# A hybrid decoder trunk: the experts' loop written out in slots of a weight tile, and score products of two heads alternated

## The chip, the core and the metric

The kernel runs on one core of a Trainium2 chip. The metric is the device time of one execution in microseconds, as the median of several. The engines' names in the rows are PE (TensorE's products), PEld (its weight loads), DVE (VectorE), ACT (ScalarE), POOL (GpSimd) and SP (the queue that issues the loads).

## What is computed

Two layers over 256 tokens of width 1024, in float32. Each layer adds a mixer, a cross attention over 256 memory tokens and a feed-forward part to `x`. The mixer has three groups: 4 mLSTM heads, a convolution over 31 taps, and 8 "FoX" heads, a causal attention whose logits get a sum of log forget gates. All heads are 64 wide. The second layer's feed-forward part is a mixture of 8 experts, of which each token uses two:

```python
def forgetting_attention(q, k, v, log_f):
    ...
        logits = jnp.einsum("bhqd,bhkd->bhqk", qi, kh) + ci[..., None] - c[:, :, None, :]
        logits = jnp.where(pi[:, None] >= kpos[None, :], logits, -jnp.inf)
        p = jax.nn.softmax(logits, axis=-1)
        return jnp.einsum("bhqk,bhkd->bhqd", p, vh)

def swiglu(h, w_gate, w_up, w_down):
    a = jnp.einsum("bsd,df->bsf", h, w_gate)
    u = jnp.einsum("bsd,df->bsf", h, w_up)
    return jnp.einsum("bsf,fd->bsd", jax.nn.silu(a) * u, w_down)

def moe_swiglu(h, router_w, w_gate, w_up, w_down):
    logits = jnp.einsum("bsd,de->bse", h, router_w).astype(jnp.float32)
    top_v, top_i = lax.top_k(logits, TOP_K)
    top_w = jax.nn.softmax(top_v, axis=-1)
    gates = jnp.sum(jax.nn.one_hot(top_i, N_EXPERTS, dtype=jnp.float32) * top_w[..., None], axis=-2)
    y = jnp.zeros(h.shape, jnp.float32)
    for e in range(N_EXPERTS):
        y = y + gates[..., e:e + 1] * swiglu(h, w_gate[e], w_up[e], w_down[e]).astype(jnp.float32)
```

The inner width of an expert is 2816. In the mLSTM too the scores of a head are products of queries and keys over 64 channels, weighted by gates.

## The kernel before

**Weights.** All weights come from memory in tiles of 128 x 2048 float32 (1 MB), in one list that `weight_order` makes. `load` (L150) takes a free staging tile and issues the load on SP; the staging has four tiles (`STAGES[0]`), for the experts three more (`STAGES[1]`) and the spare tiles named `wsp`, four of them. A product is exact enough only when its operands are split into a high part of fewer bits and the rest: `halve` (L159) makes from a tile the high half `wh` by a ScalarE copy (L165) and the low half `wl` by a VectorE subtraction (L169), each in two pieces of 128 x 1024; a staging tile is free again after its last subtraction. `w(key)` (L193) hands out the next tile of the list and lets the splitting run `split_ahead` = 2 tiles ahead.

**Experts.** The experts are worked through in eight places, 0 to 7. The tokens that belong to an expert are gathered by products with one-hot matrices `oh`, and its results are scattered back by products with the transposed ones. The even places are long, with 128 token slots: `expert` (L1194) with three products for each piece of weights (`mm3`: low x high, high x low, high x high). The odd places are short, with 64: `short` (L1234) puts the high and the low half of its tokens side by side into 128 columns, so that two products do. Each expert has 11 chunks of 256 inner channels; a chunk needs three weight tiles, two of gate and up (`eg`, 8 pieces of 512 columns) and one of down (`ed`, 4 pieces). After the products with gate and up of a chunk, a long expert does the silu (`es`, L1228), the product with up (L1229), two transposes (`et`, L1201) and the split `ehh`, `ehl`. A short one copies the result (`eg`, ACT L1276), adds the two halves and turns them in one go by products with `comb` (`et`, L1246), and then does silu (`es`, L1248), product (L1249) and split (L359, L363). The products with down follow a chunk or two later.

**What sets the order.** The code of a chunk is written as one flow; `behind` (L1155) lets turns, down products and scatters of earlier chunks come one chunk later each, and `at(fc)` (L1325) starts the gather of the next group of places (`prepare`, L1284) at chunk 3 and goes on with it, two of the eight columns per chunk. From this flow a scheduler makes each engine's order of instructions, by priority and by what it reckons to be ready. Each engine then runs its instructions in that fixed order and waits where an input is not there.

**Attention.** `attend` calls `scores(h)` for each head in turn. In `fox` (L658) this makes for each of two query blocks i a product of queries and keys (L668, 64 rows, 128 or 256 columns), the gate bias (L669) and the causal mask (L670), all added up in one PSUM tile `fs`. The heads 2p and 2p+1 lie in the two halves of the 128 rows of `fq` and `fk`. `mlstm` (L737) does its two score products (L755, 256 columns; L756, 128) for one head after the other.

Of the kernel before, what the change touches and what calls it, by code (L numbers as in the profile page):

```python
# [35 lines left out]
STAGES = (4, 3)  # L36
HALVES = 5
# [38 lines left out]
class Trunk:  # L76
# [7 lines left out]
    def __init__(self, ctx, tc, a, out):  # L84
        self.ctx, self.tc, self.nc, self.a, self.out = ctx, tc, tc.nc, a, out
        self.order = self.weight_order()
        self.loaded, self.ready = [], {}
        self.nload = self.nsplit = self.nused = 0
        self.mark = self.hold = self.kept = None
        self.split_ahead = 1  # L90
        self.cut = CUT[0]
        self.build()


    def weight_order(self):
# [3 lines left out]
        for l in range(DEPTH):  # L99
# [26 lines left out]
            lead = 3 if l % 2 == 0 else 6  # L126
# [31 lines left out]

    def halve(self, slot, st):  # L159

        nc, tc = self.nc, self.tc
        wh, wl = [Halves(*[self.wp.tile([P, 1024], F32R, name=n) for _ in range(2)]) for n in ("wh", "wl")]
# [37 lines left out]


    def build(self):
# [6 lines left out]
        self.wp = pool("wp", HALVES)  # L209
# [77 lines left out]
        with tc.tile_pool(name="emid", bufs=1) as self.md, tc.tile_pool(name="ewkb", bufs=2) as self.wb, \  # L287
                tc.tile_pool(name="wst2", bufs=STAGES[1]) as wst2:
            self.free += [slot(wst2)] * STAGES[1]
            
            self.xg = [self.big("xg", shape=(P, 2 * KD * P)) for _ in range(2)]
            self.spare()
            self.kept = self.spare()
            self.moe(0, 1)
# [363 lines left out]
    def fox(self, cat, fq, fk, fv):  # L658
        nc = self.nc
        po = {}  # L660

        def scores(h):
            hp, r = h // 2, slice((h % 2) * 64, (h % 2) * 64 + 64)
            ps = self.psum(name="fs")
            for i in range(NT):
                n = (i + 1) * P
                o = ps[:, 0:128] if i == 0 else ps[:, 128:384]
                nc.tensor.matmul(o, fq[r, hp, i * P:(i + 1) * P], fk[r, hp, 0:n], start=True, stop=False)  # L668
                nc.tensor.matmul(o, self.pick(4 + h), self.ahl[:, 0:n], start=False, stop=False)  # L669
                nc.tensor.matmul(o[:, n - P:n], self.identb, self.mask_up, start=False, stop=True)  # L670
            return ps, ((0, 128), (128, 384)), 1.0
# [64 lines left out]
    def mlstm(self, cat, qk, v1, so, nw):  # L736
# [5 lines left out]
        for h in range(5):  # L742
            if h < 4:
                r = slice((h % 2) * 64, (h % 2) * 64 + 64)
                q, kk = qk[r, h // 2, :], qk[r, 2 + h // 2, :]
# [8 lines left out]
                ps = self.psum(name="ms")  # L754
                nc.tensor.matmul(ps[:, 0:256], kk[:, 0:128], q, start=True, stop=True)  # L755
                nc.tensor.matmul(ps[:, 256:384], kk[:, 128:256], q[:, 128:256], start=True, stop=True)  # L756
# [334 lines left out]
    def moe(self, j, l):  # L1091
# [23 lines left out]
        def gather(lists, xg):  # L1115
# [8 lines left out]
            xr = wb.tile([P, len(lists)], F32, name=f"xr{len(lists)}")  # L1124

            def steps():
                for k in range(KD):
                    ks = slice(k * P, (k + 1) * P)
                    ps = self.psum(name="xg")
                    for s in range(2):  # L1130
                        for i in range(NT):
                            nc.tensor.matmul(ps[:, lo:lo + w], hm[1 - s][:, i, ks], ohs[:, i, lo:lo + w],
                                             start=s == 0 and i == 0, stop=s == 1 and i == NT - 1)
                    at = [slice(m * P + (C if short else 0), (m + 1) * P) for m, (_, short) in enumerate(lists)]
                    for t, c in zip(xg, at):
                        self.split_hi(t[:, k, 0], ps[:, c], norm.w[:, k:k + 1])
                    for t, c in zip(xg, at):
                        self.split_lo(t[:, k, 0], t[:, k, 1], ps[:, c], norm.w[:, k:k + 1])
                    if k % 2:
                        yield 1.0  # L1140
                ps = self.psum(name="xr")
                for m in range(len(lists)):
                    for i in range(NT):
                        nc.tensor.matmul(ps[:, m:m + 1], oh[:, i, m, :].bitcast(F32), rms[:, i:i + 1],
                                         start=i == 0, stop=i == NT - 1)
                nc.vector.tensor_copy(xr, ps[:, 0:len(lists)])
                yield 1.0

            return xg, xr, steps()


# [42 lines left out]
        def expert(gu, dn, x, xr, oh, gate, at=lambda fc: None, pre=()):  # L1194
# [22 lines left out]
            for fc in range(NFC):  # L1217
# [7 lines left out]
                if fc == 0:  # L1225
                    run(pre)
# [5 lines left out]
                at(fc)  # L1232

        def short(gu, dn, x, xr, oh, gate, at):  # L1234
# [3 lines left out]
            ps = [self.psum(name="ed") for _ in range(2)]  # L1238
# [4 lines left out]
            def turn(fc, g):  # L1243
                pt = self.psum((P, 4, C), "et")
                for b in range(4):
                    nc.tensor.matmul(pt[:, b, :], g[:, b * P:(b + 1) * P], comb, start=True, stop=True)  # L1246
                s = wb.tile([P, 256], F32, name="es")[:, 0:2 * C].rearrange("p (k t) -> p k t", t=C)
                nc.scalar.activation(s, pt[:, 0:2, :], AF.Silu)  # L1248
                nc.vector.tensor_tensor(s, s, pt[:, 2:4, :], op=ALU.mult)  # L1249
                h = wb.tile([P, 2, P], F32R, name="ehh", bufs=3).rearrange("p k (s t) -> p k s t", t=C)  # L1250
                self.split(h[:, :, 0, :], h[:, :, 1, :], s)
                later(lambda: down(fc, h))

            def down(fc, h):
                wh, wl = dn(fc)
                for n in range(2):
                    for k in range(2):
                        fs = slice(k * 1024 + n * 512, k * 1024 + (n + 1) * 512)
                        for w in (wl, wh):
                            nc.tensor.matmul(ps[n], h[:, k].rearrange("p s t -> p (s t)"), w[:, fs], start=fc == 0 and k == 0 and w is wl,  # L1260
                                             stop=fc == NFC - 1 and k == 1 and w is wh)
                if fc == NFC - 1:
                    evacuate(ps, oh, gate)

            for fc in range(NFC):
                pg = self.psum(name="eg")
                for hf in range(2):
                    wh, wl = gu(fc, hf)
                    for k in range(4):
                        c = hf * 4 + k  # L1270
                        fs = slice(k * 512, (k + 1) * 512)
                        for w in (wl, wh):
                            nc.tensor.matmul(pg, both[:, c], w[:, fs], start=c == 0 and w is wl,  # L1273
                                             stop=c == KD - 1 and w is wh)
                g = wb.tile([P, 512], F32, name="eg", bufs=1)
                nc.scalar.activation(g, pg, AF.Copy)  # L1276
                behind()
                turns.append(lambda fc=fc, g=g: turn(fc, g))
                at(fc)

        groups = {}
        lists = (pos, None)

        def prepare(n):  # L1284
# [3 lines left out]
            for i in range(NT):  # L1288
                for m, q in enumerate(places):
# [192 lines left out]
```

## Time and profile before

| what | value |
|---|---|
| median of 3 runs | 1386.63 us (1386.36 to 1388.93) |
| profiled execution, its own time | 1390.3 us |
| its span | 1388.5 us |
| PE busy | 1324.8 us, 95% of the span |
| DVE busy | 1175.7 us, 85% |
| ACT busy | 949.5 us, 68% |
| experts' loop, first product to last | 603.7 to about 1373 us |
| places 0 to 7 begin at | 603.7, 699.5, 783, 889.3, 978, 1080.5, 1171.2, 1274 us |

The busy shares are means over stages with different limits, so they are to be read by stretch. A place begins where its first gate and up product starts. The 1.8 us between span and own time lie around the span and are taken as given.

### The profile page before, as it was taken

Reading aid. Unit: us, or ns where it says so; the run is one execution under the profiler, and the core shown is the slowest. Engines: PE = TensorE matmul, PEld = TensorE weight load, DVE = VectorE, ACT = ScalarE, POOL = GpSimd, SP = SyncE. Lnnn points to the kernel's source line nnn. Section 1 sums busy time; section 2 is a strip of 40 time slices with the busy share of each in tenths; the row PEclk is TensorE's granted clock in tenths of the full one; section 3 lists DMA queues with packets and bytes.
Section 4 is the critical chain, followed back from the end, with each engine's and each line's share of the span. In section 5 each row is a group of like instructions: output and inputs, shape, how many; then the busy total and the mean of one; then the engine's idle time right before and its main releaser. Section 6 shows DMA issues by size and latency. Waiting matters only on the chain.

```text
span 1388.5 us, 20513 instructions
## 1 busy us (share of the span) xinstructions
PE 1324.8 (95%) x7257; PEld 1090.6 (79%) x7257; DVE 1175.7 (85%) x2059; ACT 949.5 (68%) x1501; POOL 8.1 (1%) x30
## 2 busy tenths in 40 slices
PE   9999999999999999989999989998999989999985
PEld 8878989999989778778886768866788766787663
DVE  7988876666678878689999989999999998989997
ACT  7565575444455555668799867878777787777884
POOL 0000100000000000000000000000000000000000
PEclk9999999999999999979999999999999999999998
DMA  8423626555544315669999988999999999999970
GB/s 315 173 73 116 217 92 213 182 184 185 190 177 152 122 61 182 237 235 343 337 373 391 421 323 321 353 382 380 370 347 335 357 367 389 333 341 361 337 300 33
DMA packets 67566, 368.05 MB, mean 265 GB/s; under 512 B 5744, under 2 KB 6000, under 8 KB 38016
## 3 DMA queue, kind: packets, MB, share of 16 engines
q1 hardware_dynamic: 67136, 365.59, 71.1%
q8 instruction: 59, 0.97, 0.3%
q0 software_dynamic: 320, 1.08, 0.2%
q14 instruction: 51, 0.42, 0.1%
HBM read 365.60 MB, written 1.05 MB: 264 GB/s over the span
## 4 chain that ended last, share of the span: by engine, by line
PE 71%; DVE 12%; DMA 10%; ACT 4%; issue 3%; DVEq 0%; SPq 0%; ACTq 0%
DVE wl L169 9%; PE fm L349 6%; PE fm L351 6%; PE fm L350 6%; PE eg L1273 6%; PE eg L350 5%; PE eg L349 5%; PE eg L351 5%; DMA wst<-in_moe_gu_dram 4%; DMA wst<-in_moe_w_down_dram 2%; ACT wh L165 2%; PE ed L349 2%; PE ed L351 2%; PE ed L350 2%; PE ed L1260 2%
## 5 line engine op out<-in xcount | busy, mean ns | idle before, releaser
L169 DVE TENSOR_TENSOR wl<-wst,wh 128x512 fp32r<-128x512 f32 (+1 forms) x668 | 614.0, 955 | 116.2 <-ACT wh L165 113.8
L165 ACT ACTIVATE wh<-wst 128x1024 fp32r<-128x1024 f32 x502 | 513.2, 1058 | 178.7 <-PE fm L351 90.8
L169 DVE TENSOR_TENSOR wl<-wsp,wh 128x1024 fp32r<-128x1024 f32 x188 | 222.7, 1221 | 18.8 <-ACT wh L165 16.7
L349 PE MATMUL fm<-hTh,wl 128*128 128x256 f32 x736 | 207.7, 282 | 0.7 <-DVE wl L169 0.7
L350 PE MATMUL fm<-hTl,wh 128*128 128x256 f32 x736 | 206.8, 281 | 0.0
L351 PE MATMUL fm<-hTh,wh 128*128 128x256 f32 x736 | 206.4, 280 | 0.0
L165 ACT ACTIVATE wh<-wsp 128x1024 fp32r<-128x1024 f32 x188 | 190.2, 1053 | 16.7 <-PE eg L351 7.5
L1273 PE MATMUL eg<-wl,xs 128*128 128x512 f32 x352 | 149.2, 424 | 12.2 <-DVE wl L169 11.6
L350 PE MATMUL eg<-wl,xg 128*128 128x512 f32 x352 | 141.9, 403 | 2.8 <-DVE wl L169 2.6
L349 PE MATMUL eg<-wh,xg 128*128 128x512 f32 x352 | 141.6, 402 | 0.0
L351 PE MATMUL eg<-wh,xg 128*128 128x512 f32 x352 | 140.0, 398 | 0.0
L349 PEld LDWEIGHTS fm<-hTh,wl 128*128 128x128 f32 x736 | 138.7, 188 | 1.6 <-DVE wl L169 0.9
L350 PEld LDWEIGHTS fm<-hTl,wh 128*128 128x128 f32 x736 | 138.6, 188 | 0.8 <-issue 0.2
L351 PEld LDWEIGHTS fm<-hTh,wh 128*128 128x128 f32 x736 | 138.9, 189 | 0.0
L1273 PE MATMUL eg<-wh,xs 128*128 128x512 f32 x352 | 138.4, 393 | 0.0
L1273 PEld LDWEIGHTS eg<-wl,xs 128*128 128x128 f32 x352 | 66.3, 188 | 41.5 <-DVE wl L169 19.0
L1260 PE MATMUL ed<-wl,ehh 128*128 128x512 f32 x176 | 76.7, 436 | 17.8 <-DVE wl L169 15.4
L350 PEld LDWEIGHTS eg<-wl,xg 128*128 128x128 f32 x352 | 66.9, 190 | 21.2 <-DVE wl L169 6.9
L349 PEld LDWEIGHTS eg<-wh,xg 128*128 128x128 f32 x352 | 67.0, 190 | 15.9 <-ACT wh L165 0.8
L351 PEld LDWEIGHTS eg<-wh,xg 128*128 128x128 f32 x352 | 66.7, 189 | 15.3
L1273 PEld LDWEIGHTS eg<-wh,xs 128*128 128x128 f32 x352 | 66.5, 189 | 10.0
L1260 PEld LDWEIGHTS ed<-wl,ehh 128*128 128x128 f32 x176 | 33.0, 187 | 48.7 <-DVE wl L169 35.9
(338 smaller groups left out, 2185.8 us busy)
## 6 DMA issues: line engine op xcount, KB each, us to landing
wst<-in_moe_gu_dram SPq DMA_DIRECT2D x114, 1024.0 KB, 7.0
wsp<-in_moe_gu_dram SPq DMA_DIRECT2D x62, 1024.0 KB, 7.0
wst<-in_moe_w_down_dram SPq DMA_DIRECT2D x56, 1024.0 KB, 6.9
wsp<-in_moe_w_down_dram SPq DMA_DIRECT2D x32, 1024.0 KB, 7.2
wst<-in_ffn_gu_dram SPq DMA_DIRECT2D x22, 1024.0 KB, 4.9
wst<-in_w_in_fm_dram SPq DMA_DIRECT2D x16, 1024.0 KB, 4.9
wst<-in_ffn_w_down_dram SPq DMA_DIRECT2D x11, 1024.0 KB, 5.0
wst<-in_w_in_tm_dram SPq DMA_DIRECT2D x8, 1024.0 KB, 5.2
```

The source lines that it names most:

```text
L165: self.halved = nc.scalar.activation(wh[:, s], st[:, s], AF.Copy)
L169: nc.vector.tensor_tensor(wl[:, s], st[:, s], wh[:, s].bitcast(F32), op=ALU.subtract)
L349: nc.tensor.matmul(out, ll, rh, start=start, stop=False)
L350: nc.tensor.matmul(out, lh, rl, start=False, stop=False)
L351: nc.tensor.matmul(out, lh, rh, start=False, stop=stop)
L1260: nc.tensor.matmul(ps[n], h[:, k].rearrange("p s t -> p (s t)"), w[:, fs], start=fc == 0 and k == 0 and w is wl, stop=fc == NFC - 1 and k ...
L1273: nc.tensor.matmul(pg, both[:, c], w[:, fs], start=c == 0 and w is wl, stop=c == KD - 1 and w is wh)
```

## The change

**Experts' loop.** In the loop of layer 1, ScalarE, VectorE and TensorE no longer get their order from the scheduler but from the order of the code (`manual_schedule`). The code is laid out in slots, one for each weight tile. `slot` issues in a fixed pattern: for ScalarE the steps posted at "act", the first half of the copy for the tile after next, the steps posted at "act mid", the second half; for VectorE half a subtraction for the next tile, the steps posted at "dve mid", the other half; for TensorE half of the tile's products, the steps at "pe mid", the other half, the steps at "pe". `post(n, where, step)` puts a small step into the slot n later. Silu, product, turn and split of a chunk, the scatter of a finished expert (`leave`), the gather of the next group (`spread`, one column per slot) and the norm weights for the end (`final_weights`) are posted like this. The down products of a chunk come after the gate and up products of the next.

**Buffers.** The staging has two tiles less (`STAGES` (4, 3) to (4, 1)), `wh` gets seven half tiles and `wl` six instead of five each, and the list of the experts' tiles begins with four gate and up tiles instead of six. The gather for place 0 runs as a whole before the loop; before, half of it came inside the first chunk.

**Scores.** In `fox` the two heads of a pair get their scores together, in two PSUM tiles: bias and mask of block 0 for both, the four products of queries and keys with the heads in turns, bias and mask of block 1. `mlstm` does the score products of two heads in turns as well.

```diff
-STAGES = (4, 3)
-HALVES = 5
+STAGES = (4, 1)
+HALVES = (5, {"wh": 2, "wl": 1})
...
-            lead = 3 if l % 2 == 0 else 6
+            lead = 3 if l % 2 == 0 else 4
...
+    def slot(self, key, *products):
+        t = self.nused
+        assert self.order[t][0] == key, (self.order[t][0], key)
+        self.now += 1
+        if t + 1 < len(self.order) and t + 1 >= self.nsplit and t + 1 not in self.parts:
+            self.high(t + 1, 0)
+            self.high(t + 1, 1)
+        self.places("act")
+        self.high(t + 2, 0)
+        self.low(t + 1, 0)
+        self.places("dve mid", "act mid")
+        self.high(t + 2, 1)
+        self.low(t + 1, 1)
+        w = self.ready.pop(key)
+        products[0](*w)
+        self.places("pe mid")
+        products[1](*w)
+        self.places("pe")
+        self.nused += 1
...
+            bias(0, True)
             for i in range(NT):
...
+                for k in range(2):
+                    r = slice(k * 64, k * 64 + 64)
+                    nc.tensor.matmul(out(k, i), fq[r, h // 2, i * P:(i + 1) * P], fk[r, h // 2, 0:(i + 1) * P],
+                                     start=i == 1, stop=i == 0)
+            bias(1, False)
...
+                if h % 2 == 0:
+
+                    made = [self.psum(name="ms") for _ in range(2)]
+                    for s in range(NT):
+                        for k in range(2):
+                            r = slice(k * 64, k * 64 + 64)
+                            o = made[k][:, 0:256] if s == 0 else made[k][:, 256:384]
+                            nc.tensor.matmul(o, qk[r, 2 + h // 2, s * P:(s + 1) * P], qk[r, h // 2, s * P:T],
+                                             start=True, stop=True)
+                ps = made[h % 2]
...
+                self.post(1, "act", lambda: nc.scalar.activation(s, pg[:, 0:256], AF.Silu, scale=xr))
+                self.post(1, "dve mid", lambda: nc.vector.scalar_tensor_tensor(
+                    s, pg[:, 256:512], xr, s, op0=ALU.mult, op1=ALU.mult))
+                self.post(1, "pe", turn)
+                self.post(2, "act", lambda: self.split_hi(h[0], pt))
+                self.post(2, "dve mid", lambda: self.split_lo(*h, pt))
...
+                self.post(1, "act", lambda: nc.scalar.activation(g, pg, AF.Copy))
+                self.post(1, "pe mid", turn)
+                self.post(2, "act", lambda: nc.scalar.activation(s, pt[:, 0:2, :], AF.Silu))
+                self.post(2, "dve mid", lambda: nc.vector.tensor_tensor(s, s, pt[:, 2:4, :], op=ALU.mult))
+                self.post(2, "act mid", lambda: self.split_hi(hs[:, :, 0, :], s))
+                self.post(3, "dve mid", lambda: self.split_lo(hs[:, :, 0, :], hs[:, :, 1, :], s))
...
+        with tc.manual_schedule(engines={mybir.EngineType.PE, mybir.EngineType.Activation, mybir.EngineType.DVE}):
+            for n, places in enumerate(GROUPS):
+                oh, xg, xr = groups.pop(n)
+                for m, q in enumerate(places):
+                    def at(fc):
+                        if q == E - 1 and fc == NFC - 6:
+                            self.final_weights()
+                        if m == len(places) - 1 and fc == 2 and n + 1 < len(GROUPS):
+                            spread(n + 1)
```

On ScalarE, in a short expert (place 3), one chunk of the kernel before reads as follows (`wst` and `wsp` are staging tiles):

```order
L1248 ACTIVATE es<-et 128x128
L165 ACTIVATE wh<-wst 128x1024 x2
L1276 ACTIVATE eg<-eg 128x512
L359 ACTIVATE ehh<-es 128x2x64
L165 ACTIVATE wh<-wst 128x1024 x4
L1248 ACTIVATE es<-et 128x128
```

and of the changed kernel, from one copy of `eg` to the next:

```order
L1399 ACTIVATE eg<-eg 128x512
L222 ACTIVATE wh<-wsp 128x1024 x2
L1401 ACTIVATE es<-et 128x128
L222 ACTIVATE wh<-wsp 128x1024
L424 ACTIVATE ehh<-es 128x2x64
L222 ACTIVATE wh<-wsp 128x1024
L222 ACTIVATE wh<-wst 128x1024 x2
L1399 ACTIVATE eg<-eg 128x512
```

The silu `es` stood behind four copies, with the copy of `eg` ahead of them and two copies between it and the next; now it stands two copies behind the copy of `eg`, and its split a copy behind it.

On TensorE, at the start of the first layer's FoX heads, one head of the kernel before:

```order
L668 MATMUL fs<-fk,fq 128x128
L669 MATMUL fs<-ahl,sel 128x128
L670 LDWEIGHTS identb
L670 MATMUL fs<-mask_up,identb 128x128
L668 MATMUL fs<-fk,fq 128x256
L669 MATMUL fs<-ahl,sel 128x256
L670 LDWEIGHTS identb
L670 MATMUL fs<-mask_up,identb 128x128
```

and of the changed kernel, the second head's part of block 0, the four products of both heads, and the first head's part of block 1:

```order
L741 MATMUL fs<-ahl,sel 128x128
L742 LDWEIGHTS identb
L742 MATMUL fs<-mask_up,identb 128x128
L748 MATMUL fs<-fk,fq 128x128 x2
L748 MATMUL fs<-fk,fq 128x256 x2
L741 MATMUL fs<-ahl,sel 128x256
L742 LDWEIGHTS identb
L742 MATMUL fs<-mask_up,identb 128x128
```

The products of queries and keys, one at a time between biases before, now stand four in a row, those of the two heads in turns.

## Rows read from the trace of the kernel before

**Rows 1.** Busy by stretch (us): span, PE, PEld, DVE, ACT, POOL, PEclk, DMA, GB/s.

```profile
699.50:783.00 83.50, 81.47 (x374) 60.63 (x372) 82.25 (x92) 77.46 (x101) 0.00 (x0) 1.00 0.99 390
783.00:889.30 106.30, 101.86 (x460) 81.87 (x459) 97.00 (x122) 79.37 (x108) 0.00 (x0) 0.98 0.91 340
889.30:978.00 88.70, 80.63 (x365) 59.86 (x364) 83.51 (x97) 72.96 (x100) 0.00 (x0) 1.00 0.98 381
978.00:1080.50 102.50, 101.23 (x467) 81.51 (x467) 95.95 (x117) 79.95 (x110) 0.00 (x0) 1.00 0.95 348
1080.50:1171.20 90.70, 81.36 (x365) 59.70 (x365) 83.74 (x95) 72.90 (x100) 0.00 (x0) 1.00 0.98 372
1171.20:1274.00 102.80, 101.47 (x464) 80.80 (x462) 92.09 (x108) 75.20 (x101) 0.00 (x0) 1.00 0.95 344
603.70:1274.00 670.30, 643.82 (x2925) 502.32 (x2924) 618.22 (x727) 532.91 (x712) 0.00 (x0) 0.99 0.95 356
```

**Rows 2.** Timeline of ACT (start, length): first, last `eg` of places 1 and 7.

```profile
703.80 0.57 ACT L1276 ACTIVATE eg<-eg 128x512 f32<-128x512 f32 x1
...
780.37 0.60 ACT L1276 ACTIVATE eg<-eg 128x512 f32<-128x512 f32 x1 [0.19 <-PE eg L1273]
...
1278.51 0.60 ACT L1276 ACTIVATE eg<-eg 128x512 f32<-128x512 f32 x1 [0.84 <-PE eg L1273]
...
1363.49 0.59 ACT L1276 ACTIVATE eg<-eg 128x512 f32<-128x512 f32 x1
```

**Rows 3.** Timeline of ACT and DVE in place 3, two chunks following each other.

```profile
948.82 0.28 ACT L1248 ACTIVATE es<-et 128x128 f32<-128x128 f32 x1 [1.53 <-PE et L1246]
...
957.00 0.28 ACT L1248 ACTIVATE es<-et 128x128 f32<-128x128 f32 x1 [1.53 <-PE et L1246]
...
950.08 1.23 DVE L169 TENSOR_TENSOR wl<-wst,wh 128x1024 fp32r<-128x1024 f32 x1 [0.66 <-ACT wh L165]
```

**Rows 4.** Busy by stretch, 40 us in place 1, columns of rows 1.

```profile
750.00:790.00 40.00, 39.66 (x178) 28.79 (x178) 39.56 (x44) 36.61 (x48) 0.00 (x0) 1.00 1.02 420
```

**Rows 5.** The page's DMA issues: KB each, median us from issue to landing.

```profile
wst<-in_moe_gu_dram SPq DMA_DIRECT2D x114, 1024.0 KB, 7.0
```

**Rows 6.** Timeline of PE, score products of the first fox head, layer 0.

```profile
63.37 0.49 PE L668 MATMUL fs<-fk,fq 64*128 64x128 f32 x2
63.78 0.33 PE L669 MATMUL fs<-ahl,sel 128*128 128x128 f32 x1
...
64.11 0.70 PE L668 MATMUL fs<-fk,fq 64*128 64x256 f32 x2
64.74 0.38 PE L669 MATMUL fs<-ahl,sel 128*128 128x256 f32 x1
```

**Rows 7.** Timeline of PE, mlstm's score products: alone, and beside another head's.

```profile
108.44 0.70 PE L755 MATMUL ms<-qk 64*128 64x256 f32 x2
108.98 0.38 PE L756 MATMUL ms<-qk 64*128 64x128 f32 x2
109.29 0.44 PE L679 MATMUL po<-pT,fv 128*64 128x256 f32 x2
...
119.14 0.37 PE L756 MATMUL ms<-qk 64*128 64x128 f32 x1
...
119.99 0.38 PE L432 MATMUL nrow<-ndg,ones 128*128 128x128 f32 x1
```

**Rows 8.** Busy by stretch, both layers' attention, columns of rows 1.

```profile
63.20:115.70 52.50, 52.50 (x323) 41.26 (x322) 45.78 (x122) 31.60 (x82) 1.64 (x5) 1.00 0.30 103
453.90:495.00 41.10, 41.10 (x236) 31.42 (x235) 33.21 (x89) 25.02 (x70) 0.20 (x2) 0.96 0.28 102
```

**Rows 9.** Timeline of ACT and DVE in place 4: silu and its product.

```profile
1002.71 0.48 ACT L1228 ACTIVATE es<-eg,xr 128x256 f32<-128x256 f32 x1 [1.68 <-PE eg L351]
...
1003.43 0.48 DVE L1229 SCALAR_TENSOR_TENSOR es<-eg,xr,es 128x256 f32<-128x256 f32 x1
```

**Rows 10.** The page's costliest groups: busy us, mean ns, idle before.

```profile
L165 ACT ACTIVATE wh<-wst 128x1024 fp32r<-128x1024 f32 x502 | 513.2, 1058 | 178.7 <-PE fm L351 90.8
```

More of the change, by code (lines that the diff above doesn't have):

```diff
@@ L1124, in gather, with products @@
             xr = wb.tile([P, len(lists)], F32, name=f"xr{len(lists)}")
+            at = [slice(m * P + (C if short else 0), (m + 1) * P) for m, (_, short) in enumerate(lists)]
+            ps = {}
+            def products(k):
+                ps[k] = self.psum(name="xg")
+                for s in range(2):
+                    for i in range(NT):
+                        nc.tensor.matmul(ps[k][:, lo:lo + w], hm[1 - s][:, i, k * P:(k + 1) * P], ohs[:, i, lo:lo + w],
+                                         start=s == 0 and i == 0, stop=s == 1 and i == NT - 1)
@@ L1126, in steps, with keep_scales @@
+            def keep_scales():
+                nc.vector.tensor_copy(xr, ps["r"][:, 0:len(lists)])
             def steps():
                 for k in range(KD):
[L1128 to L1145, printed above, removed]
@@ L1254, in down, with part @@
[L1254 to L1263, printed above, removed]
+            def part(pg, hf, k, wh, wl):
+                c = hf * 4 + k
+                fs = slice(k * 512, (k + 1) * 512)
+                for w in (wl, wh):
+                    nc.tensor.matmul(pg, both[:, c], w[:, fs], start=c == 0 and w is wl, stop=c == KD - 1 and w is wh)
@@ L1265, in short, with expert_slots @@
+        def expert_slots(q, kind, x, xr, oh, gate, at):
+            ps = [self.psum(name="ed") for _ in range(2)]
+            part, chain, down = kind(x, xr)
             for fc in range(NFC):
@@ L1267, in short, with downs, lists_of @@
                 for hf in range(2):
[L1268 to L1278, printed above, removed]
+                    self.slot(("gu", l, q * NFC + fc, hf), *[
+                        lambda wh, wl, k=k: [part(pg, hf, j, wh, wl) for j in (k, k + 1)] for k in (0, 2)])
+                h = chain(pg)
+                def downs(fc=fc, h=h):
+                    steps = [lambda wh, wl, n=n: [
+                        down(ps, h, n, k, fc == 0 and k == 0, fc == NFC - 1 and k == 1, wh, wl) for k in range(2)]
+                        for n in range(2)]
+                    self.slot(("dn", l, q * NFC + fc), *steps)
+                    if fc == NFC - 1:
+                        leave(ps, oh, gate)
                 at(fc)
+                if pending:
+                    pending.pop(0)()
+                pending.append(downs)
         groups = {}
-        lists = (pos, None)
-        def prepare(n):
+        def lists_of(n):
             places = GROUPS[n]
```

258 lines of the change are left out of this document (180 added, 78 removed).

## The prediction

> **What bounds the kernel now.** I read the engines' busy time by stretch first, one stretch per expert. The long experts (places 2, 4, 6) keep TensorE busy for 101.86, 101.23 and 101.47 us of 106.3, 102.5 and 102.8 [rows 1]: TensorE is the bound there, and the time lost in a long expert is what its stretch has over about 101.5. The short experts (places 1, 3, 5) keep TensorE busy for only about 81 us and VectorE for 82.25, 83.51 and 83.74 us [rows 1]. VectorE is busy for 98.5% of the first (82.25 of 83.5), but for 94% of the second and 92% of the third: the same work takes 83.5 us once and 88.7 and 90.7 us after. Place 7 shows it too: from the first copy of a gate and up result to the last, ten chunks on, 85.0 us pass (1278.51 to 1363.49), in place 1 only 76.6 (703.80 to 780.37) [rows 2].
>
> Why the later short experts are slower is in ScalarE's rows. The silu `es` waits 1.53 us for TensorE's transposes `et`, and the same 1.53 again one chunk, 8.18 us, later [rows 3]. ScalarE takes its instructions in order, so the copies `wh` behind that silu start late, and VectorE's next subtraction waits 0.66 us for one of them [rows 3]. TensorE in turn waits for the subtraction. It is a loop through three engines that repeats in each chunk, and no engine is full in it. In place 1 the scheduler happened to find an order without it. In place 2 the extra 4.4 us (106.3 less 101.86) lie in one stop of TensorE, not in each chunk.
>
> Transfers are not the limit: while VectorE is 99% busy (39.56 of 40.0 us) the loads move 420 GB/s [rows 4], more than the 356 GB/s mean of the experts' loop [rows 1], and one MB lands 7.0 us after its issue [rows 5] with about nine tiles issued ahead of their use.
>
> **Order by hand, short experts.** In the changed order the silu of a chunk stands behind two `wh` copies, at the start of the slot after that in whose middle TensorE does the transposes that feed it. A short chunk has three slots, so a third of 7.7 us: 2.6 us. The silu then finds its input ready, the 1.53 us go, and with them the 0.66. What is late next is VectorE itself: its busy time of 83.7 us is the floor. (TensorE needs less: a long expert's 464 records come to 101.47/464 = 0.22 us each, so the 365 of a short one, among which more are narrow, to 80 us at most [rows 1].) The ceiling is 83.7/0.985 = 85.0, the share that place 1 reached. I take the middle, 84.4. That gives 83.5 − 84.4 = −0.9 for place 1, 88.7 − 84.4 = 4.3 for place 3, 90.7 − 84.4 = 6.3 for place 5, and for place 7 85.0 − 76.6 − 0.9 = 7.5: together **17.2** us. ScalarE has 73 to 77 us of work in these stretches [rows 1], which fits in 84.4 with 7 us to spare; this is the cover that the copies need. What else moves in a short expert (the scatter of the expert before, the gather steps, the norm weights of place 7, which now start three chunks earlier) keeps its instructions and so is in the busy times already; SP's queue has the same loads in the same order of tiles, each still issued when a subtraction has freed a staging tile.
>
> **Order by hand, long experts.** The floor is TensorE's 101.5 us. Places 2, 4 and 6 have 106.3, 102.5 and 102.8, so 4.8 + 1.0 + 1.3 = **7.1** us. The 4.8 of place 2 goes only if the spreading of the next group's gather over slots keeps TensorE fed: the `oh` marks now stand one per slot, and each of the eight gather steps in a slot of its own. VectorE is the next in line with 92 to 97 us [rows 1].
>
> **Start and end of the loop.** Place 0 now gets its whole gather before the loop instead of half of it inside, and the copies run two tiles ahead in a fixed order; the staging shrinks from 11 tiles to 9 and the lead of gate and up tiles from 6 to 4. Nine tiles at 2.6 us per tile are 23 us of cover against the 7.0 us landing, so the smaller staging costs nothing; if the landing became three times as long, it would cost. For the start I bound the cost between 0 and 2 us, and the end, where small steps now wait for empty slots, at −1.5 to +1.5. I take 0 for both.
>
> **Score products of two heads.** Before, each fox head does its 128-column product (0.41 us to the next start, 63.37 to 63.78) and its 256-column product (0.63 us, 64.11 to 64.74) alone, between bias and mask products [rows 6]. These products contract over 64 rows only, and two heads lie in different halves of the rows. What happens if two such products follow each other is shown once in mlstm: a 256-column and a 128-column product alone take 0.54 and 0.31 us (108.44, 108.98, 109.29), and where another head's 128-column product stands directly ahead, all three take 0.85 us (119.14 to 119.99) [rows 7]. The added one was free. So a fox pair can hide up to 0.41 + 0.63 = 1.04 us, eight pairs in two layers 8.3; four mlstm pairs can hide 0.85 each less the 0.31 that is already hidden, 2.2. The upper bound is 10.5 us. The lower is 0: the added order makes a pair's softmax start later, and VectorE has 45.78 us of 52.5 in the first layer's stretch and 33.21 of 41.1 in the second's [rows 8]. As TensorE is full in both stretches, most of its saving should show, until the convolution's taps on VectorE end last. I take 6 us, just over the middle. The softmax of the second head of a pair has nothing to wait for that the first one's doesn't, so I see no loss.
>
> **Sum.** 17.2 + 7.1 + 0 + 6 = 30.3 us. The profiled execution took 1390.3 us by its own time, so it becomes 1360.0; the median of the runs is 1386.63, 3.7 less, and becomes 1356.3.
>
> **Rivals.**
> (A) A new in-order wait takes the place of the old one. The fixed order has waits too: TensorE's transposes stand in the middle of a slot at whose start ScalarE copies `eg` for them, and ScalarE may still be at a `wh` copy then. Then the short experts stay near 88.7: place 1 loses 5.2, place 5 gains 2.0, place 7 gains 7.5 − 4.3 = 3.2, place 3 nothing, together 0, and only 7.1 + 6 stay: 1373.5 us. For it: places 3, 5 and 7 all fell into such a loop, with the same instructions as place 1. Against it: place 1 shows that the work fits without one.
> (M) The memory can't give more. All experts' weights come in at a mean of 356 GB/s [rows 1]; were this a limit, the loop would keep its 670 us and only the attention's 6 remain: 1380.6. Against it are the 420 GB/s over 40 us [rows 4], and the loads' wait for free staging tiles rather than the other way round. The Trainium skill (DMA: Bandwidth & Descriptors, Where 436 GB/s comes from) says that the memory side binds at about 358 GB/s per core; the loop's mean looks like it, but the 420 GB/s of this trace are above it, so the measurement decides. By that rule the loop could not shorten.
> (Z) The pairs bring nothing, VectorE being next: 1362.3.
> (S) Slower. In a long expert ScalarE's silu (0.48), VectorE's product (0.48) and one subtraction ahead of that (1.23) [rows 3, 9] must end within the slot in which TensorE does the transposes: 2.2 of 101.5/33 = 3.08 us, a margin of 0.9. If the silu comes behind two copies that are themselves late (2 × 1.06 [rows 10]), TensorE stands for 1.2 us in each of 44 long chunks, as nothing can be moved ahead of the transposes now: 53 us, so 1356.3 + 53 = 1409. It decides the sign from 1.6 us of lateness on (0.9 + 30.3/44). Against it: ScalarE is busy for only 75 to 80 of about 102 us there [rows 1], so it should run ahead.
> That the change doesn't do what it says can be left out for the pairs: in the order of the products below the heads alternate. For the loop it is rival A.
>
> **How the numbers follow.** The forecast has 0.64, rival A 0.13, M 0.06, Z 0.07, S 0.06; a better case, in which the shorts come to VectorE's floor (4 × 0.7 more), the attention to its bound (4.5 more) and the loop's ends save 3 to 5, has 0.04: 1344. A measurement of this kernel tells 0.2%, 2.8 us, from no change. Faster has all but S and a small part of M and of A with a piece of S: 0.90. Slower is S and a mixed case, 0.07, within 0.2% 0.03. The range goes from 1343 (the better case) to 1376 (rival A with a place more lost at the start); M and S lie outside.
>
> **What would show it.** Right: four short stretches of about 84 us with VectorE at 98% or more, silus without a wait for `et`, long stretches near 101.5 with TensorE full, two fox heads' products that start within 0.1 us of each other, and attention stretches 2 to 4 us shorter. Wrong: short stretches with a repeated wait of ScalarE or VectorE; loads waiting for nothing while subtractions wait for a load (M); TensorE idle ahead of `et` in the long chunks (S); attention as long as before with VectorE full (Z).

## The result, and the profile after

The changed kernel takes **1344.2 us** (median, 1342.6 to 1346.1) against 1387.4 us before: a ratio of 0.969, 95% interval 0.967 to 0.971. That is 43 us faster; the forecast was 30 us, and the result lies just inside the lower end of its range. The two profiled executions differ by more, 1390.3 to 1343.7; on why, see the attention below.

The experts' loop first, busy time by place. Columns as in [rows 1]; the last line runs to the end of the span:

```profile
590.75:688.39 97.64, 97.64 (x447) 79.62 (x448) 84.24 (x107) 74.11 (x101) 0.00 (x0) 0.98 0.90 331
688.39:771.66 83.27, 78.26 (x369) 60.24 (x368) 83.27 (x95) 74.61 (x102) 0.00 (x0) 1.00 0.99 393
771.66:871.71 100.05, 100.05 (x466) 81.70 (x464) 93.39 (x119) 76.28 (x106) 0.00 (x0) 1.00 0.96 361
871.71:954.99 83.28, 78.21 (x370) 60.17 (x369) 83.26 (x95) 74.61 (x102) 0.00 (x0) 1.00 1.00 397
954.99:1054.97 99.98, 99.98 (x466) 81.64 (x464) 93.36 (x119) 76.28 (x106) 0.00 (x0) 1.00 0.96 362
1054.97:1138.23 83.26, 78.23 (x369) 60.17 (x368) 83.26 (x95) 74.59 (x102) 0.00 (x0) 1.00 1.01 398
1138.23:1237.69 99.46, 99.46 (x461) 81.23 (x460) 90.90 (x109) 74.14 (x98) 0.00 (x0) 1.00 0.97 366
1237.69:1341.80 104.11, 84.70 (x403) 64.90 (x401) 95.52 (x139) 77.86 (x112) 0.00 (x0) 0.95 0.70 269
```

Each short place (1, 3, 5) takes 83.3 us and VectorE is busy for all of it; each long place (2, 4, 6) takes 99.5 to 100.0 and TensorE is busy for all of it. Before, a short place took 83.5 to 90.7 with VectorE at 92 to 98.5%, and a long one 102.5 to 106.3 [rows 1]. The loads come in at 393 to 398 GB/s in the short places.

Ten chunks of place 7 on ScalarE, first and last `eg`, to compare with the 85.0 us of [rows 2]:

```profile
1242.05 0.59 ACT L1399 ACTIVATE eg<-eg 128x512 f32<-128x512 f32 x1
...
1319.57 0.57 ACT L1399 ACTIVATE eg<-eg 128x512 f32<-128x512 f32 x1
```

77.5 us. And the silu, its surroundings and the next copies in place 3 (timeline of ScalarE), as in [rows 3]:

```profile
908.74 0.57 ACT L1399 ACTIVATE eg<-eg 128x512 f32<-128x512 f32 x1
...
911.11 0.27 ACT L1401 ACTIVATE es<-et 128x128 f32<-128x128 f32 x1
911.27 1.05 ACT L222 ACTIVATE wh<-wst 128x1024 fp32r<-128x1024 f32 x1
912.89 0.31 ACT L424 ACTIVATE ehh<-es 128x128 fp32r<-128x128 f32 x1 [0.57 <-DVE es L1402]
```

The silu has no bracket: here it waits for nothing, where 1.53 us stood before; its split `ehh` behind it waits 0.57 us for VectorE's product. The waits summed over the loop, up to the last gate and up products, tell it best (engine, line, what it waited for: us in total, times, longest). Before:

```profile
ACT es L1248 <- PE et L1246: 42.1, 29, 2.2
ACT es L1228 <- PE eg L351: 37.4, 43, 2.9
...
DVE wl L169 <- ACT wh L165: 42.6, 91, 3.0
```

After, of ScalarE and of VectorE:

```profile
ACT es L1360 <- PE eg L416: 55.4, 43, 1.9
ACT ehh L424 <- PE et L1358: 36.6, 40, 1.6
ACT ehh L424 <- DVE es L1402: 30.7, 37, 2.1
...
ACT es L1401 <- PE et L1397: 3.8, 8, 0.6
```

```profile
DVE wl L230 <- ACT wh L222: 3.8, 2, 3.4
```

ScalarE still waits, and in sum not much less: all its waits in these stretches come to 152 us before and 132 after. In the long chunks the silus wait longer (55.4 us against 37.4) and the splits too (36.6 against 12.3); in the short ones the wait for `et` has all but gone (3.8 us against 42.1), but the splits now wait 30.7 us for VectorE's products. What has gone is the wait of VectorE's subtractions for its copies: 42.6 us in 91 places have become 3.8 in 2.

The attention: from the first fox score product to the first output product, layers 0 and 1, of the kernel before and after (columns as in [rows 1]):

```profile
63.37:121.04 57.67, 57.67 (x358) 45.66 (x358) 49.13 (x128) 35.36 (x91) 1.64 (x5) 1.00 0.35 126
453.87:507.77 53.90, 52.88 (x302) 40.04 (x300) 43.64 (x113) 32.95 (x87) 0.20 (x2) 0.97 0.27 98
```

```profile
63.70:117.55 53.85, 53.04 (x363) 43.22 (x362) 48.74 (x126) 34.96 (x91) 1.65 (x5) 1.00 0.38 134
448.20:494.98 46.78, 45.97 (x305) 35.52 (x303) 43.44 (x113) 31.55 (x84) 0.20 (x2) 1.00 0.31 113
```

3.8 us less in layer 0 and 7.1 in layer 1. Not all of the 7.1 is the change's: the profile of before got a granted clock of 0.97 in that stretch, and a run below with the same attention code at 1.00 takes 52.1 us there, not 53.9. This is part of why the profiles differ by 46.6 us and the medians by 43.

### The profile page after: what moved, and what is told of

It is laid out like the page before. It is cut to its first block, busy times and chain, and to the rows that moved or that the text cites. A ratio compares the mean times of both kernels' runs of the same rounds, so it can differ in the third digit from the quotient of the medians.

```text
span 1341.8 us, 20592 instructions
## 1 busy us (share of the span) xinstructions
PE 1293.8 (96%) x7257; PEld 1083.8 (81%) x7257; DVE 1162.5 (87%) x2059; ACT 937.5 (70%) x1501; POOL 7.5 (1%) x30
## 4 chain that ended last, share of the span: by engine, by line
PE 71%; DVE 17%; issue 6%; ACT 4%; DMA 1%; DVEq 0%; SPq 0%; ACTq 0%
DVE wl L230 9%; PE eg L414 6%; PE eg L416 6%; PE eg L415 6%; PE fm L414 5%; PE fm L416 5%; PE fm L415 5%; PE ed L1410 4%; PE ed L414 3%; PE ed L416 3%; PE ed L415 3%; PE et L1397 2%; DVE wl L172 2%; PE pr L414 2%; PE pr L415 2%
## 5 line engine op out<-in xcount | busy, mean ns | idle before, releaser
L230 DVE TENSOR_TENSOR wl<-wst,wh 128x1024 fp32r<-128x1024 f32 x294 | 347.9, 1220 | 3.4 <-ACT wh L222 3.4
L222 ACT ACTIVATE wh<-wst 128x1024 fp32r<-128x1024 f32 x294 | 295.3, 1052 | 3.2 <-PE eg L416 3.2
L172 DVE TENSOR_TENSOR wl<-wst,wh 128x512 fp32r<-128x512 f32 x332 | 217.2, 687 | 86.8 <-ACT wh L168 86.5
L230 DVE TENSOR_TENSOR wl<-wsp,wh 128x1024 fp32r<-128x1024 f32 x230 | 274.5, 1220 | 0.3 <-ACT wh L222 0.3
L168 ACT ACTIVATE wh<-wst 128x1024 fp32r<-128x1024 f32 x166 | 173.4, 1062 | 144.4 <-PE fm L416 87.5
L222 ACT ACTIVATE wh<-wsp 128x1024 fp32r<-128x1024 f32 x230 | 234.6, 1053 | 0.8 <-PE eg L416 0.8
L1386 PE MATMUL eg<-wl,xs 128*128 128x512 f32 x352 | 140.2, 398 | 0.3
L1410 PE MATMUL ed<-wl,ehh 128*128 128x512 f32 x176 | 80.5, 457 | 20.1 <-DVE wl L230 17.7
L415 PEld LDWEIGHTS eg<-wl,xg 128*128 128x128 f32 x352 | 66.7, 190 | 13.5
```

The costliest lines, as they stand in the source:

```text
L168: self.halved = nc.scalar.activation(wh[:, s], st[:, s], AF.Copy)
L172: nc.vector.tensor_tensor(wl[:, s], st[:, s], wh[:, s].bitcast(F32), op=ALU.subtract)
L222: self.nc.scalar.activation(wh[:, s], st[:, s], AF.Copy)
L230: self.nc.vector.tensor_tensor(wl[:, s], st[:, s], wh[:, s].bitcast(F32), op=ALU.subtract)
L415: nc.tensor.matmul(out, lh, rl, start=False, stop=False)
L1410: nc.tensor.matmul(ps[n], h[:, k], w[:, fs], start=start and w is wl, stop=stop and w is wh)
```

## The experiments

**The two parts apart.** First the kernel before with the new `fox` and `mlstm` put in, nothing else changed:

> The kernel before with the new fox and mlstm alone; the experts' loop is as before. Theory: the pairs bring the loop's start 11 to 13.8 us forward and the loop takes its 670 us as before, so about 1387.4 - 12 = 1375 us. Rival 1 (what the two traces show ahead of the loop is partly the lower granted clock, 0.97 against 1.00, that the second layer's attention of the profile of before happened to get): 8 to 9 us, 1379. Rival 2 (the pairs' gain is eaten by the loop, whose order the scheduler makes anew): 1384 to 1388.

Measured: 1377.5 us, ratio 0.992 (0.991 to 0.994), so 10.7 us less, between the 12 of the theory and the 8 to 9 of rival 1; the loop takes about its old time. Then the reverse, the changed kernel with the old `fox` and `mlstm`:

> The changed kernel with the old fox and mlstm; the experts' loop in slots stays. Theory: the two parts add up, so 1344.2 + 12 = 1356 us, with places 1, 3 and 5 at 83.3 us each and 2 and 4 at 100.0. Rival (the parts share something): under 1350 or over 1362.

Measured: 1354.5 us, ratio 0.976 (0.974 to 0.978): 33.7 us from the loop alone, and 10.3 from the pairs on top. 10.7 + 33.7 = 44.4 against the 43 to 44 of both: the parts add up, and the places 1 to 6 of this kernel take what they take in the changed one. Its attention, the old code at full clock:

```profile
63.28:120.75 57.47, 57.47 (x358) 45.49 (x358) 48.96 (x128) 35.36 (x91) 1.64 (x5) 1.00 0.36 127
453.75:505.88 52.13, 51.11 (x301) 38.47 (x300) 43.28 (x113) 32.83 (x87) 0.20 (x2) 1.00 0.29 100
```

So the pairs save 57.47 − 53.85 = 3.6 and 52.13 − 46.78 = 5.4 us in these stretches; the rest of the 10.3 lies around them.

**Is it the turns?** The heads one after the other within each group:

```diff
-            for i in range(NT):
-                for k in range(2):
+            for k in range(2):
+                for i in range(NT):
                     r = slice(k * 64, k * 64 + 64)
```

> The changed kernel, but the four score products of a pair stand head by head (128 and 256 columns of the first, then of the second) and not in turns; in mlstm too. Theory (products in turns run at the same time): most of the hiding is lost, 0.6 of 1.04 us for each of 8 fox pairs and 0.5 for each of 4 mlstm pairs, so 7 us: 1351. Rival (the gain is that products over 64 rows stand together and TensorE changes less often between 64 and 128 rows): nothing is lost, 1344 to 1346.

Measured: 1344.2 us; nothing is lost. I took this for the rival at first, but the trace says otherwise. In this kernel's order on TensorE the second product is the first head's 256 columns and only the third the second head's 128. All that began in the first 0.3 us of a group (63.44 to 63.76, groups by line and shape; two records for each product):

```profile
L748 PE MATMUL fs<-fk,fq 64*128 64x128 f32 x4 | 0.5, 322 | 0.0
```

Both heads' 128-column products run, and no product of 256 columns yet: the third in the order has started ahead of the second. So TensorE does not strictly start its products in the order that it is given, unlike what the section on the kernel before says of each engine. A group takes as long as in the changed kernel. So the products overlap with or without turns, and the experiment could not tell the two theories apart. This one does:

```diff
-r = slice(k * 64, k * 64 + 64)
+r = slice(0, 64)
```

in `fox` and `mlstm`: the second head of a pair computes the first one's scores again, so both heads' products lie in the same 64 rows.

> The changed kernel, but both heads of a pair read the first half of the rows for queries and keys (the second head's scores are then those of the first; the products' sizes and order stay). Theory (products in the two row halves run at the same time): the four products of a group take twice as long, since one head's two products alone hold TensorE for about 0.8 us in the records of the changed kernel; 8 fox and 4 mlstm pairs lose 0.6 to 0.85 us each, 7 to 10 us: 1351 to 1354, about what the kernel with the old attention takes (1354.5). Rival (grouping alone pays, as fewer changes between 64 and 128 rows): 1344 to 1346.

Measured: 1348.8 us, 4.6 more than the changed kernel. The four products of the first group with what stands ahead of them, on TensorE's timeline, in the changed kernel:

```profile
63.84 0.23 PE L742 MATMUL fs<-mask_up,identb 128*128 128x128 bf16 x1
63.88 0.30 PE L741 MATMUL fs<-ahl,sel 128*128 128x128 f32 x1
64.03 0.23 PE L742 MATMUL fs<-mask_up,identb 128*128 128x128 bf16 x1
64.19 0.93 PE L748 MATMUL fs<-fk,fq 64*128 64x128 f32 x8
65.04 0.38 PE L741 MATMUL fs<-ahl,sel 128*128 128x256 f32 x1
```

and with both heads in the same rows:

```profile
63.45 1.57 PE L748 MATMUL fs<-fk,fq 64*128 64x128 f32 x8
64.96 0.38 PE L741 MATMUL fs<-ahl,sel 128*128 128x256 f32 x1
```

0.85 us from the first product to the next bias, against 1.51. Products in different halves of the rows do run at the same time, and it hides 0.66 us per group, as the theory had it. But 12 groups would make 7.9 us, and 4.6 are seen; and against the old attention (1354.5) 5.7 us remain that this kernel, without any overlap, has gained too. That is the grouping. Both show in the stretches of the attention as well; this kernel's are

```profile
62.96:119.44 56.48, 55.85 (x363) 45.80 (x362) 49.20 (x129) 35.10 (x91) 1.65 (x5) 1.00 0.37 130
451.28:500.66 49.38, 49.25 (x306) 38.67 (x304) 43.59 (x113) 32.19 (x86) 0.20 (x2) 1.00 0.30 106
```

Together 105.9 us, between 109.6 for the old attention and 100.6 for the changed kernel: 3.7 for the grouping and 5.2 for the overlap here, where the medians have 5.7 and 4.6. The two parts are of about one size, and their exact shares stay open.

What a group saves can be estimated. With p for one head's two products and e for each time that TensorE goes from 128 rows to 64 and back, [rows 6] gives p + 2e = 0.41 + 0.63 = 1.04 and the row above 2p + e = 1.51, so e = 0.19 and p = 0.66 us (worked out, not seen directly). The 0.85 us of a group whose heads overlap, and the 0.54 + 0.31 of one mlstm head alone [rows 7], are p + e = 0.85 too. Three such changes less in each of 8 fox pairs and one in each of 4 mlstm pairs are 28 × 0.19 = 5.3 us. This is an estimate and not the whole: e leaves out that a 64-row product starts 0.16 us after a mask product (64.03 to 64.19) and a 128-row one only 0.04 (63.84 to 63.88), and it counts every saving as if it were on the path. Whether the change of shape itself takes the time, or the load of weights that stands open there, no run here separates. Theory and rival were each about half of it.

**Is it the buffers, the slots or the order?** The buffers alone, in the kernel before:

```diff
-STAGES = (4, 3)
-HALVES = 5
+STAGES = (4, 1)
+HALVES = (5, {"wh": 2, "wl": 1})
```

> The kernel before with the changed kernel's buffers alone: seven wh and six wl half tiles, nine staging tiles instead of eleven; list of tiles, order and attention as before. Theory (order pays, not buffers): 1384 to 1391, no change. Rival (buffers pay): 1355 to 1375.

Measured: 1389.0 us, ratio 0.999 (0.998 to 1.000): no change in the whole. By place it is not nothing, since the scheduler makes a new order for these buffers: place 2 takes 4.0 us less (102.3), places 3 and 7 take 2.3 and 1.2 more. Next, the changed kernel whose loop the scheduler orders again:

```diff
-        with tc.manual_schedule(engines={mybir.EngineType.PE, mybir.EngineType.Activation, mybir.EngineType.DVE}):
+        with nullcontext():
```

> The changed kernel without the fixed order: the same code in slots with the same buffers, but the scheduler orders the experts' loop on all engines again. Theory (the fixed order itself pays): the scheduler puts copies behind waiting silus again, short places come to 86 to 90 us and the time to 1360 to 1376. Rival (writing the steps in slots and the buffers pay, whoever sets the order): 1344 to 1350.

Measured: 1369.3 us, 25 us of the loop's 33 gone, as the theory had it. Places 3 and 5 of this kernel, and its largest wait of VectorE in places 1 to 7:

```profile
874.50:963.58 89.08, 83.68 (x370) 58.20 (x369) 83.14 (x97) 73.09 (x100) 0.00 (x0) 1.00 0.97 375
...
1065.05:1153.75 88.70, 83.77 (x370) 58.18 (x369) 82.78 (x95) 73.10 (x100) 0.00 (x0) 1.00 0.98 373
```

```profile
DVE wl L230 <- ACT wh L222: 29.8, 65, 1.5
```

Places 3 and 5 are back at 89 us and VectorE waits for copies again; the long places take 1.4 to 1.5 us more than in the changed kernel. Place 1 is an exception: it takes 82.7 us, for once the scheduler found a good order. So most of the gain is the fixed order's. About 8 us stay without it (1377.5 with the pairs alone, 1369.3 here), from the code in slots with its buffers; 4.7 of them lie in place 2, whose one stop of TensorE (4.2 us before, a gather product waiting for its `oh` marks) is gone here too.

**What in the order?** The same order with the copies one tile closer to their subtractions:

```diff
-        if t + 1 < len(self.order) and t + 1 >= self.nsplit and t + 1 not in self.parts:
-            self.high(t + 1, 0)
-            self.high(t + 1, 1)
         self.places("act")
-        self.high(t + 2, 0)
+        self.high(t + 1, 0)
         self.low(t + 1, 0)
         self.places("dve mid", "act mid")
-        self.high(t + 2, 1)
+        self.high(t + 1, 1)
```

> The changed kernel, but in each slot ScalarE copies the next tile instead of the one after it, so a copy stands in the same slot as its subtraction, behind the same silus and waits. Theory (what pays is that the copies run two tiles ahead, so ScalarE's waits for TensorE don't reach VectorE): a short chunk loses about 1.3 us since the split behind the silu then holds up a copy that is wanted at once, 15 us in each of the places 1, 3, 5 and 7, and a long chunk 0.3 us, 3 us in each of the others: 1344 + 60 + 12 = 1416, at least 1375. Rival (the slots themselves pay, the lead is spare): 1344 to 1350.

Measured: 1473.4 us, 6% slower than the kernel before. Places 3 and 4:

```profile
914.92:1021.60 106.68, 85.91 (x368) 61.08 (x368) 86.86 (x96) 77.13 (x102) 0.00 (x0) 0.97 0.88 326
1021.60:1130.25 108.65, 105.25 (x465) 79.40 (x464) 93.09 (x118) 76.18 (x106) 0.00 (x0) 1.00 0.89 319
```

and VectorE's wait in place 3 and in place 4:

```profile
DVE wl L230 <- ACT wh L222: 19.2, 23, 1.4
DVE wl L230 <- ACT wh L222: 15.3, 20, 1.3
```

The direction was right, the size not: a short place loses 23 to 25 us, not 15, and a long one 6 to 9, not 3. I had counted one late copy in a chunk; there are two, in the short chunks and in the long ones (23 and 20 in 11 chunks). And a late copy feeds on itself: in place 3 TensorE now waits 14.6 us for subtractions before gate and up products, and ScalarE's splits wait 15.6 us for VectorE's products where they waited 7.5. Half a tile of lead back (the second half of the next tile, then the first half of the one after):

> The changed kernel with a copy lead of one and a half tiles: in each slot ScalarE copies the second half of the next tile and then the first half of the one after it. Theory (what pays is the lead of the copies over their subtractions, by which ScalarE's waits don't reach VectorE): between the lead of two (1344) and of one (1473), and nearer to two, since half a slot is 1.25 to 1.5 us and the wait that reached VectorE with a lead of one was about 2.3 us in a short chunk (25 us in 11 chunks) and 0.6 in a long: about 1.0 us in each of 44 short chunks, nothing in the long ones, 1390 (1365 to 1410). Rival (a lead of any length is enough once the order is fixed, and a lead of one failed for its place behind the silus): 1344 to 1350.

Measured: 1357.7 us, below the range that the theory gave (1365 to 1410) and above the rival's. The short places take 86.5 us, and VectorE's waits are many but short (places 1 to 6; 0.3 us each):

```profile
DVE wl L230 <- ACT wh L222: 23.3, 79, 0.5
```

18 of the 23.3 us lie in the long places, which take 99.7 to 100.2 us, hardly more than in the changed kernel: there VectorE has time to spare, and the waits cost next to nothing. In a short place nine waits of 0.2 us cost most of the 3.2 us.

Losses of 0, 13.5 and 129 us at leads of 2, 1.5 and 1 tiles: the lead is what the fixed order buys. It can be seen directly, as the time from the end of a copy to the start of its subtraction (mean over place 3, worked out from the starts and ends of both): 1.6 us in the changed kernel, 0.6 and 0.3 at the shorter leads, 0.7 where the scheduler orders the slots, 0.5 in the kernel before. Place 1 of the kernel before, which had next to nothing to gain, had 2.2. Last, the half tiles:

```diff
-HALVES = (5, {"wh": 2, "wl": 1})
+HALVES = (5, {})
```

> The changed kernel with five wh and five wl half tiles instead of seven and six. Theory (what pays is a copy lead of two tiles, for which five wh halves are just enough when the first half of the tile in use is free early): 1344 to 1352. Rival (the added half tiles pay): back to what the loop took before, 1375 to 1378.

Measured: 1354.5 us, 10 more, just outside what the theory gave. A short place takes 85.4 us; here ScalarE's copies wait for TensorE to release a half tile (places 1 to 6, down products of the short places):

```profile
ACT wh L222 <- PE ed L1410: 29.7, 30, 1.8
```

But VectorE's subtractions wait for copies no more than in the changed kernel (4.8 us in 2 waits over the loop, against 3.8 in 2). What reaches VectorE is the silu that stands behind such a copy. One chunk of place 3, on ScalarE and VectorE:

```profile
912.48 1.06 ACT L222 ACTIVATE wh<-wsp 128x1024 fp32r<-128x1024 f32 x1 [1.16 <-PE ed L1410]
913.45 0.26 ACT L1401 ACTIVATE es<-et 128x128 f32<-128x128 f32 x1
913.74 0.29 DVE L1402 TENSOR_TENSOR es<-es,et 128x128 f32<-128x128 f32 x1
```

VectorE's product starts when the silu ends (913.71). From this product to the next one's start a chunk takes 7.41 us (913.74 to 921.15), in the changed kernel 7.22 (905.36 to 912.58): 0.19 in each of 11 chunks is the 2.1 us of a short place. So with the scheduler's order the buffers changed nothing in the whole, and under the fixed order they are worth 10 us: they keep ScalarE from waiting for TensorE ahead of a silu that VectorE wants.

**More of the same for the values.** The products of probabilities and values, which write 64 columns of TensorE's output per head, in pairs too, and the score groups kept in one piece:

```diff
+                for i in range(NT):
+                    for k in range(2):
+                        o = po["o", h // 2][k * 64:k * 64 + 64, i * P:256]
+                        g = h - 1 + k
+                        nc.tensor.matmul(o, fv[:, i, g * 64:g * 64 + 64], pts[k][:, i * 256:256 + i * P],
+                                         start=i == 0, stop=i == 1)
```

> The changed kernel, in which the products of probabilities and values of two fox heads come together too, with the heads in turns (their results lie in the two halves of 64 columns of TensorE), and each group of four score products is kept in one piece. Theory (halves of the columns run at the same time as halves of the rows do, and what stands together changes TensorE's shape less often): one head's two value products hold TensorE for 0.85 us in the changed kernel, so up to 0.85 us less for each of 8 pairs; half of the groups stay mixed with others and some of it isn't on the path, so 3 to 6 us less: 1338 to 1341. Rival (column halves don't run at the same time): 0 to 2 us from the grouping, 1342 to 1344; or the later first head costs as much: 1345.

Measured: 1343.9 us, ratio 0.967 (0.966 to 0.969): the same as the changed kernel, the time that the rival gave, but not for its reason. The overlap is there. One head's two products in the changed kernel, and four products of two heads here, on TensorE's timeline:

```profile
81.20 0.65 PE L759 MATMUL po<-pT,fv 128*64 128x256 f32 x2
81.69 0.38 PE L760 MATMUL po<-pT,fv 128*64 128x128 f32 x2
82.00 0.33 PE L741 MATMUL fs<-ahl,sel 128*128 128x128 f32 x1
...
85.79 0.87 PE L765 MATMUL po<-pT,fv 128*64 128x256 f32 x8
86.63 0.33 PE L706 MATMUL pt<-ident,pe 128*128 128x128 f32 x1
```

0.84 us for four, against 0.80 for one head's two. In four of the eight pairs all four products stand together; in the changed kernel two pairs already did. But the stretches of the attention don't shrink with TensorE's busy time:

```profile
63.05:117.36 54.31, 52.23 (x369) 42.74 (x368) 49.52 (x130) 34.76 (x91) 1.65 (x5) 1.00 0.40 136
448.61:496.57 47.96, 45.54 (x311) 35.38 (x310) 43.91 (x115) 32.41 (x87) 0.20 (x2) 1.00 0.35 121
```

97.8 us of products in 102.3, against 99.0 in 100.6 in the changed kernel: TensorE now waits more, for ScalarE's exponentials and for the convolution on VectorE. In the second layer:

```profile
PE lm L791 <- DVE hc L782: 1.2, 1, 1.2
PE pt L706 <- ACT pe L697: 1.1, 2, 0.7
```

There the changed kernel has 0.3 and 0.5 us. So the saving on TensorE is used up. No kernel run here beats the changed one by more than can be told.

## Why the prediction was right, and where it was short

**What bounds the kernel:** right. The short places are VectorE's, the long ones TensorE's, and both are now full.

**The cause in the short places:** right, and shown: where copies follow their subtractions more closely, or where the scheduler orders them, VectorE waits for them and the places grow; buffers alone change nothing in the whole. One step was put too narrowly. The prediction had ScalarE's wait disappear, and VectorE's with it. The short silus' wait for `et` has all but gone (3.8 us), but the splits behind them wait instead (30.7 us), and in the long chunks silus and splits wait longer than before; it costs nothing, because the copies behind them are two tiles ahead of their use. The lead, not the absence of waits, is the gain. The prediction named the lead only in passing.

**The sizes in the loop** were the first term that was off: 17.2 + 7.1 + 0 = 24.3 us forecast against 33.7 in the run of the loop alone. The two traces show where (33.7 us from the loop's first product to the end of the span, 784.8 to 751.1). The floors were too high: places 1, 3 and 5 take 83.3, not 84.4, and places 2, 4 and 6 take 100.0, 100.0 and 99.5, not 101.5, which is 3 × 1.1 + 1.5 + 1.5 + 2.0 = 8.3 us. Place 7's ten chunks gave the 7.5 us forecast. Busy time of a full engine was taken for what it must do; but the 101.2 us for 467 records became 100.0 for 466 with the same work in a steadier order, so they must have held some 1.2 us that the record doesn't show as idle; this follows from the two sums and is not seen by itself. And the middle between 83.7 and 85.0 assumed that some of VectorE's idling must stay; none did. Start and end, taken as 0 each, came to −2.6 (the loop's first product 0.8 us later after the routing, and place 0 97.6 us instead of 95.8) and +2.6 (from 25.6 to 23.0 us between the last gate and up product and the end). They cancel, but each lies beyond the bounds I gave.

**The attention** was the second: 6 us forecast, 10.3 to 10.7 measured, at the bound of 10.5. I had come down from the bound because VectorE would be next; it was not yet (43 of 47 us in layer 1), and only the further step of pairing the values ran into it. That the bound was met is luck: it is right by two errors. It counted 10.5 us of overlap, of which 4.6 show by the medians, and it had no term for the grouping, fewer changes between 64 and 128 rows, which gave 5.7. The rows held it: 0.41 us alone for a product of 128 columns, next to 0.63 for twice as many [rows 6], so 0.22 for 128 columns and 0.19 for what does not grow with them.

Together 8.3 + 4.5 = 12.8 us, which is what the forecast lacks (43.2 − 30.3 = 12.9).

**The rivals.** A did not come: no short place stays near 88.7, and the short silus' waits for the transposes come to 3.8 us in all. M did not: 393 to 398 GB/s over whole places of 83 us. The figure that the prediction named from the Trainium skill (DMA: Bandwidth & Descriptors, Where 436 GB/s comes from), about 358 GB/s per core, is no limit here. Z did not. S did not come at a lead of two. A lead of one tile is slower as well, 1473 us, but in another way than S had it: VectorE's subtractions wait for copies in every place, three quarters of the loss come from the short ones, and TensorE's waits for the silu's product ahead of `et` in the long chunks are 7.2 us in all, where S had 53. What the prediction said would show it (83 to 84 us per short place, no wait for `et`, long places full, two heads' first products 0.007 us apart) is what the trace shows.

## What to carry to other kernels

Where engines work in order and feed each other in a ring, look at which instruction stands behind a wait, and how far ahead of its use it runs: a wait is free while what is queued behind it is early, and very dear when it isn't (0, 13.5, 129 us at leads of 2, 1.5 and 1 tiles). Here the buffers paid only with an order that uses them. A full engine's busy time isn't yet its floor. And small products of another shape can cost as much for being alone as for their columns (0.19 and 0.22 us for 128 columns here): put them together, and where they use different halves of the array, near each other.

## What the runs showed of the hardware

- Two products over 64 rows each, in different halves of the rows, run at the same time (0.85 us for four, 1.51 in the same half), and they need not stand next to each other: the third in the order started ahead of the second. Products into different halves of 64 columns do so as well (0.84 us for four, 0.80 for one head's two).
- Going from products over 128 rows to products over 64 and back costs about 0.19 us, an estimate worked out from 1.04 and 1.51 us; it leaves out the 0.16 us instead of 0.04 from a mask product to the first of them.
- The loads kept 393 to 398 GB/s for 83 us at a time on one core.
